# Input sums and part of the weight splits by accumulating transfers in a two-layer streaming encoder

## Chip, cores and metric

One core of one Trainium2 chip runs the whole program. The metric is the device time of one execution in microseconds (us); lower is better. Names of engines: PE is TensorE, DVE is VectorE, ACT is ScalarE, POOL is GpSimd, SP is SyncE (it issues the loads here).

## The reference, cut to what matters

Two token groups (512 prompt frames and 64 sample frames, 576 columns in all) go through two layers with shared weights, model width 1024, hidden width 2816. Every layer is a feed-forward block, a token mixer, and a second feed-forward block, each behind a norm whose shift, scale and gate come from a vector c per group:

```
mod = (silu(c) @ ada_w[l] + ada_b[l])          # shift, scale, gate for 3 sub-layers
hh  = rmsnorm(x) * (1 + scale) + shift
x   = x + 0.5 * gate * ((silu(hh @ w_gate) * (hh @ w_up)) @ w_out)     # feed-forward, twice in a layer
x   = x + gate * mixer(hh)      # layer 0: gated DeltaNet and short conv; layer 1: stick-breaking attention
```

So there are four feed-forward blocks; here they are called F0 (layer 0, first), F1 (layer 0, second), F2 (layer 1, first) and F3 (layer 1, second). Mixer 0 stands between F0 and F1, mixer 1 (the attention) between F2 and F3.

## The kernel before

**Precision by splitting.** Activations and weights are float32, each held as a high part rounded to the matrix unit's format and a low rest: XH, XL for a block's input (8 tiles of 128 rows, 576 columns), `wh`, `wl` for a weight tile. A product takes three matmuls, wh with XH, wh with XL, wl with XH, and runs over 288 columns (one half of the frames) at a time. `w_split` makes the pair: ACT copies the source into `wh`, and DVE subtracts, `wl = source - wh`.

**Pairs.** Weights come as 512 KB grains into three `stage` buffers, two grains to a pair. In a feed-forward block one pair is one gate tile and one up tile of 128 hidden units, over both halves of the frames. A plain pair (`dense`) takes 2 tiles x 8 row blocks x 2 halves x 3 = 96 matmuls.

**Seven-product pairs.** A pair can also be done by a fast 2x2 matrix scheme (`dense7`) with seven block products in place of eight: 7 x 4 x 3 = 84 matmuls, in the order P1, P2, P6, P5, P7, P3, P4. It needs sums of weight blocks (`w_sum`: four DVE operations into `ss`), four split weight tiles (`w_tile` 0 to 3; tile 0 serves P1 and P2, tile 1 P6 and P5, tile 2 P7 and P3, tile 3 P4) and four sums of input quarters, TH and TL, made once for each block by `t_task`. P6 adds into the PSUM bank in which P1 lay, so ACT's copy of P1 (`sg<-d`) has to be done before P6 starts. Tiles 0 to 2 of a pair are prepared during the products of the pair ahead, tile 3 after its own P1; the first seven-product pair behind a stretch of plain work prepares tiles 2 and 3 itself, after its P1.

`PLAIN = (22, 10, 10, 2)` says how many of a block's 22 pairs are plain, the first ones: F0 has no seven-product pair, F1 and F2 have 12 each, F3 has 20. A block's pairs go in chunks of 8, 8 and 6, and behind each chunk stands its part of the output product (source HH, HL). The first two pairs of a block run together in `start_sub`, and `t_task` is started behind them; it must be through (`S.finish(tt)`) before the first seven-product pair.

**Modulation.** `ada_task` computes `mod` on DVE: for each of the 144 tiles a 512 KB load `aw` and two fused multiply-and-sum operations (`jk<-aw,cb`), with `every` as the least distance between tiles. Layer 0's tiles but the first two groups are computed in F0, all 72 of layer 1 in F1 and F2.

**Order.** All engines run in program order. The order is made when the program is built: a table of engine clocks (`Model`) decides at each `S.tick()`, after every third matmul, which background task is stepped next.

Of the kernel before, what the change touches and what calls it, by code (L numbers as in the profile page):

```python
# [32 lines left out]
D = 1024  # L33
# [10 lines left out]
PK = ((1,5),(0,1))  # L44
LOLAG = 0
DSH = ((2, 4, 6), (1, 4, 6))
PLAIN = (22, 10, 10, 2)
EVEN_ODD = (0, 2, 4, 6, 1, 3, 5, 7)


# [241 lines left out]
def encoder_step(ctx: ExitStack, tc: tile.TileContext, a, o):  # L292
    nc = tc.nc
    M = Model()
# [43 lines left out]
    for n, sh in SMALL:  # L338
        k = 1
# [27 lines left out]
    def seven(i):  # L367

        return i < len(pairs) and pairs[i][0][0][2] == EVEN_ODD

    ss = {}
    spool = [None]
    HB = 4 * P

    def w_split(i, src, E=V):
        n = Model.size(src)
        h, l = wsp.tile([P, 1024], F32R, name="wh"), wsp.tile([P, 1024], F32R, name="wl")
        wt.setdefault(i, []).append((h, l))
        for c in range(0, n, HB):
            A.activation(h[:, c:c + HB], src[:, c:c + HB], AF.Copy)  # L380
        E.tensor_sub(l[:, :n], src, h[:, :n].bitcast(F32))

    def w_sum(i, n):

        g0, g1 = st[i, 0], st[i, 1]
        a11, a12, a21, a22 = g0[:, :HB], g0[:, HB:], g1[:, :HB], g1[:, HB:]
        if n in (1, 3):
            ss[i, n] = spool[0].tile([P, 1024], F32, name="ss", bufs=2)
        x1, x2 = ss[i, 1], ss.get((i, 3))
        if n == 1:  # L390
            V.tensor_add(x1[:, HB:], a21, a22)
        if n == 2:
            V.tensor_sub(x1[:, :HB], x1[:, HB:], a11)
        if n == 3:
            V.tensor_sub(x2[:, :HB], a11, a21)
        if n == 4:
            V.tensor_sub(x2[:, HB:], a12, x1[:, :HB])

    def w_tile(i, n):

        if n == 0:
            w_split(i, st[i, 0])
        if n == 1:
            w_split(i, ss[i, 1])
        if n == 2:
            w_split(i, ss.pop((i, 3)))
            ss.pop((i, 1))
            st.pop((i, 0))
            w_dma()
        if n == 3:  # L410
            w_split(i, st[i, 1][:, HB:])
            st.pop((i, 1))
            w_dma()

# [78 lines left out]
    def dense7(evac):  # L493
# [43 lines left out]
                evac(n, None)  # L537
        wt.pop(i)

    def t_task(pool):  # L540

        TH[0] = pool.tile([P, 4, 4, 288], F32R, name="TH")
        TL[0] = pool.tile([P, 4, 4, 288], F32R, name="TL")
        h0, h1 = slice(0, 288), slice(288, 576)
        Hf, Lf = XH.bitcast(F32), XL.bitcast(F32)

        def parts(n, k, t, E):
            A.activation(TH[0][:, n - 1, k], t, AF.Copy)
            E.tensor_sub(TL[0][:, n - 1, k], t, TH[0][:, n - 1, k].bitcast(F32))

        new = lambda: npool.tile([P, 288], F32, name="hf", bufs=5)
        for k in range(4):
            e, o = 2 * k, 2 * k + 1
            t1, b = new(), new()
# [3 lines left out]
            t2 = new()  # L558
            V.tensor_sub(t2, Hf[:, o, h1], t1)
            V.tensor_add(t2, t2, Lf[:, o, h1])  # L560
            yield S.clock + 300.0
            parts(2, k, t2, V)
            parts(1, k, t1, V)
            t3, d = new(), new()
            V.tensor_sub(t3, Hf[:, o, h1], Hf[:, e, h1])
            V.tensor_sub(d, Lf[:, o, h1], Lf[:, e, h1])
            V.tensor_sub(t2, Hf[:, o, h0], t2)
            V.tensor_add(t2, t2, Lf[:, o, h0])
            yield S.clock + 300.0
            V.tensor_add(t3, t3, d)  # L570
            parts(3, k, t3, V)
            parts(4, k, t2, V)
            yield S.clock + 300.0
# [168 lines left out]
    def ada_cond(pool):
        cb = pool.tile([P, 2, D], F32, name="cb")
        dma(cb, bass.AP(tensor=a["c"].tensor, offset=a["c"].offset, ap=[[0, P], [D, 2], [1, D]]))
        A.activation(cb, cb, AF.Silu)
        return cb
# [34 lines left out]
    def ffn(l, s, pool, task, out):  # L781
# [5 lines left out]
        def evac7(jj):  # L787
# [27 lines left out]
            def evac(step, ps):  # L815
                if step == "P1":
                    g[0] = copy("sg", ps, 3)
                n = {"P1": 0, "P2": 1, "P6": 2}.get(step, step)
                if step == "P6":
                    g[1] = copy("sg", ps, 3)  # L820
                if n in late:
                    late.pop(n)()
                if step == "P2":
                    V.tensor_add(g[0], g[0], ps)
                if step == "P5":
                    up[0] = copy("hm", ps, 2)
# [1007 lines left out]
```

## Time and profile before

| | |
|---|---|
| median of 3 runs | 2550.49 us (2549.56 to 2550.81) |
| the profiled execution | 2550.91 us, its span 2549.2 us |
| PE busy | 2384.6 us (94%), 18556 matmuls |
| DVE busy | 1791.0 us (70%) |
| ACT busy | 986.8 us (39%) |
| POOL busy | 353.6 us (14%) |
| DMA | 277.00 MB, mean 109 GB/s |

Matmuls overlap in the trace, so a busy PE says only that it had work; a stretch is judged by how many matmuls it holds. Stretches, in us from the span's start: F0 40 to 468, mixer 0 to 905, F1 to 1334, F2 to 1779, mixer 1 to 2120, F3 to the end.

### The profile page before, as it was taken

What the parts mean: (1) busy time and instruction counts of PE and PEld (TensorE: products, weight loads), DVE (VectorE), ACT (ScalarE), POOL (GpSimd) and SP (SyncE); (2) the same over time, 40 slices, a digit from 0 to 9 for tenths busy, and PEclk for the clock granted to TensorE, in tenths of its full rate; (3) what the DMA queues carried; (4) which work ended last, traced back from release to release, by engine and by line L of the source; (5) the groups of instructions that cost most, each with busy time, mean ns of one, the idle gap of its engine ahead of it and who ended that gap; (6) DMA issues with size and microseconds to landing.
All of it is one profiled execution on the core that took longest, in us unless ns stands there. A gap on an engine that the chain in (4) does not pass through costs nothing.

```text
span 2549.2 us, 46027 instructions
## 1 busy us (share of the span) xinstructions
PE 2384.6 (94%) x18556; PEld 2304.2 (90%) x18556; DVE 1791.0 (70%) x3528; ACT 986.8 (39%) x2015; POOL 353.6 (14%) x599
## 2 busy tenths in 40 slices
PE   6999999999998979989997998999999996999998
PEld 5999999988888969989896998999888886999998
DVE  7677776687775676687877658775656667748575
ACT  4322222543222432142443314344655544525352
POOL 4000000432222310000011000002333322000001
PEclk8999999998888989999998999999999998999999
DMA  6454443322122214344331443422222221223322
GB/s 236 158 173 160 173 158 131 120 77 55 32 65 90 102 67 157 116 141 141 133 123 67 149 149 116 130 77 92 88 72 84 66 83 34 91 83 93 98 82 81
DMA packets 95399, 277.00 MB, mean 109 GB/s; under 512 B 24738, under 2 KB 27042, under 8 KB 94804
## 3 DMA queue, kind: packets, MB, share of 16 engines
q1 hardware_dynamic: 95188, 274.07, 32.5%
q8 instruction: 146, 2.39, 0.4%
q14 instruction: 65, 0.53, 0.1%
HBM read 262.52 MB, written 11.51 MB: 107 GB/s over the span
## 4 chain that ended last, share of the span: by engine, by line
PE 70%; DVE 19%; ACT 5%; issue 3%; POOL 2%; DMA 1%; SPq 0%; DVEq 0%; ACTq 0%; POOLq 0%
PE d L191 61%; PE a L191 9%; DVE hf L191 3%; DVE wl L191 3%; DVE jk L191 2%; ACT wh L191 2%; DVE iz L191 1%; DVE ss L191 1%; DVE sg L191 1%; DVE cp L191 1%; ACT sg L191 1%; DVE TL L191 1%; DVE t2k L191 1%; DVE sy L191 1%; POOL sn L191 1%
## 5 line engine op out<-in xcount | busy, mean ns | idle before, releaser
L191 PE MATMUL d<-XH,wh 128*128 128x288 f32 x2832 | 869.8, 307 | 47.6 <-ACT sg L191 16.1
L191 PE MATMUL d<-XL,wh 128*128 128x288 f32 x2832 | 850.9, 300 | 16.1 <-POOL XL L191 9.5
L191 PE MATMUL d<-XH,wl 128*128 128x288 f32 x2832 | 847.7, 299 | 0.8 <-DVE wl L191 0.8
L191 PEld LDWEIGHTS d<-XH,wh 128*128 128x128 f32 x2832 | 544.6, 192 | 62.7 <-ACT sg L191 16.8
L191 PEld LDWEIGHTS d<-XL,wh 128*128 128x128 f32 x2832 | 545.3, 193 | 23.2 <-POOL XL L191 15.2
L191 PEld LDWEIGHTS d<-XH,wl 128*128 128x128 f32 x2832 | 544.3, 192 | 1.7 <-DVE wl L191 1.5
L191 DVE TENSOR_TENSOR wl<-stage,wh 128x1024 fp32r<-128x1024 f32 (+3 forms) x319 | 354.9, 1117 | 169.4 <-ACT wh L191 167.8
L191 ACT ACTIVATE wh<-stage 128x1024 fp32r<-128x1024 f32 (+3 forms) x389 | 334.6, 878 | 274.4 <-PE d L191 240.9
L191 PE MATMUL d<-HH,wh 128*128 128x288 f32 x1408 | 416.3, 296 | 0.0
L191 PE MATMUL d<-HL,wh 128*128 128x288 f32 x1408 | 416.0, 295 | 0.0
L191 PE MATMUL d<-HH,wl 128*128 128x288 f32 x1408 | 414.2, 294 | 0.3 <-DVE wl L191 0.3
L191 DVE SCALAR_TENSOR_TENSOR jk<-aw,cb 128x1024 bf16<-128x1024 f32 x272 | 339.2, 1247 | 4.8
L191 DVE SCALAR_TENSOR_TENSOR x<-d,mod,x 128x64 f32<-128x64 f32 (+2 forms) x384 | 146.7, 413 | 208.4 <-PE d L191 207.0
L191 POOL TENSOR_TENSOR acc<-acc,sq 128x288 f32<-128x288 f32 x72 | 58.4, 812 | 1653.3 <-ACT sq L191 1239.7
L191 PEld LDWEIGHTS d<-HH,wl 128*128 128x128 f32 x1408 | 264.5, 188 | 0.6 <-DVE wl L191 0.6
L191 PEld LDWEIGHTS d<-HL,wh 128*128 128x128 f32 x1408 | 264.2, 188 | 0.7 <-DVE HL L191 0.7
L191 PEld LDWEIGHTS d<-HH,wh 128*128 128x128 f32 x1408 | 264.1, 188 | 0.0
L191 PE MATMUL d<-TH,wh 128*128 128x288 f32 x704 | 214.2, 304 | 46.9 <-ACT sg L191 46.9
L191 PE MATMUL d<-TL,wh 128*128 128x288 f32 x704 | 212.4, 302 | 0.0
L191 PE MATMUL d<-TH,wl 128*128 128x288 f32 x704 | 212.1, 301 | 0.0
L191 ACT ACTIVATE HH<-hm 128x288 fp32r<-128x288 f32 x176 | 74.7, 445 | 295.1 <-DVE hm L191 295.1
L191 PEld LDWEIGHTS d<-TH,wh 128*128 128x128 f32 x704 | 136.9, 194 | 51.1 <-ACT sg L191 50.4
(319 smaller groups left out, 3181.6 us busy)
## 6 DMA issues: line engine op xcount, KB each, us to landing
stage<-in_w SPq DMA_DIRECT2D x301, 512.0 KB, 3.6
aw<-in_ada SPq DMA_DIRECT2D x136, 512.0 KB, 4.4
stage<-in_w SPq DMA_DIRECT2D x36, 384.0 KB, 3.1
stage<-in_w SPq DMA_DIRECT2D x8, 320.0 KB, 3.0
x<-in_x SPq DMA_DIRECT2D x4, 576.0 KB, 7.2
xd<-x SPq DMA_DIRECT2D x1, 2304.0 KB
x<-xd SPq DMA_DIRECT2D x1, 2304.0 KB
out_k<-kf SPq DMA_DIRECT2D x8, 288.0 KB, 4.4
```

Of the source, the lines that this page charges most:

```text
L191: r = real(*args, **kw)
```

## The change

- `t_task` no longer forms the four input sums on DVE (56 operations on 128x288). ACT copies four quarters of XH into TL, and ten accumulating transfers issued by POOL (`acc_dma`, a transfer that adds its source into its destination) add the other quarters to them. ACT then copies each sum to TH and DVE subtracts once for each quarter. The scheme's signs are turned so that only sums are needed; the weight sums change add for subtract. XH and XL are stored by quarters, so that a quarter is one run of 1152 elements in each partition.
- In F1 and F2 (`S2M`), the rests of weight tiles 2 and 3 are made by ACT and a transfer: ACT writes `wl = -source` rounded, and `acc_dma` adds the source.
- `PLAIN` becomes (22, 6, 6, 6): F1 and F2 get 16 seven-product pairs, F3 16.
- Modulation tiles: 48 in F0, 48 in F1 and F2 (as far as they reach), 24 in mixer 1, 8 in F3; `cb` (silu of c, broadcast) stays in place for the whole program, `aw` has fewer buffers. The output tile of the end shares its place with TH.
- The scratch of POOL's transfers grows from 512 to 2048 bytes.

```diff
-PLAIN = (22, 10, 10, 2)
+PLAIN = (22, 6, 6, 6)
...
-    XH = base.tile([P, 8, NT], F32R, name="XH")
-    XL = base.tile([P, 8, NT], F32R, name="XL")
+    XH = Quarters(base.tile([P, 2, 2, 4, 288], F32R, name="XH"))
+    XL = Quarters(base.tile([P, 2, 2, 4, 288], F32R, name="XL"))
+    cb = base.tile([P, 2, D], F32, name="cb")
...
-    def w_split(i, src, E=V):
+    def w_split(i, src, E=V, by_dma=False):
...
             A.activation(h[:, c:c + HB], src[:, c:c + HB], AF.Copy)
+        if by_dma:
+            A.activation(l[:, :n], src, AF.Copy, scale=-1.0)
+            acc_dma(l[:, :n].bitcast(F32), src)
+            return
         E.tensor_sub(l[:, :n], src, h[:, :n].bitcast(F32))
...
-            w_split(i, ss.pop((i, 3)))
+            w_split(i, ss.pop((i, 3)), by_dma=S2M[0])
...
-            w_split(i, st[i, 1][:, HB:])
+            w_split(i, st[i, 1][:, HB:], by_dma=S2M[0])
...
+    def acc_dma(out, in_):
+
+        nc.gpsimd.dma_start(out, in_, accum_op=OP.add)
+        M.issue("POOL", [out], [in_], 1000.0)
...
     def t_task(pool):
...
-            V.tensor_sub(t1, Hf[:, e, h1], Hf[:, e, h0])
-            V.tensor_sub(b, Lf[:, e, h1], Lf[:, e, h0])
-            V.tensor_add(t1, t1, b)
...
+        def parts(n):
+            A.activation(TH[0][:, n], Tf[n], AF.Copy)
+            V.tensor_sub(TL[0][:, n], Tf[n], TH[0][:, n].bitcast(F32))
+
+        for n, (par, half) in enumerate(((0, 0), (1, 1), (0, 1), (1, 0))):
+            A.activation(TL[0][:, n], H(par, half), AF.Copy)
+        yield S.clock
+        for x, y in ((L(0, 0), L(0, 1)), (H(0, 1), H(1, 1)), (L(0, 1), L(1, 1))):
+            acc_dma(Tf[0], x)
+            acc_dma(Tf[2], y)
+        acc_dma(Tf[1], L(1, 1))
+        acc_dma(Tf[3], L(1, 0))
+        acc_dma(Tf[1], Tf[0])
+        yield M.ready(Tf[2]) + 2000.0
+        parts(2)
+        yield M.ready(Tf[1]) + 1000.0
+        acc_dma(Tf[3], Tf[1])
+        yield S.clock + 2000.0
+        parts(0)
+        yield M.ready(Tf[3]) + 2000.0
+        parts(1)
+        yield S.clock + 2000.0
+        parts(3)
...
-        at = S.spawn(ada_task(ap, cb, [(0, j) for j in range(2, 9)], 5600.0))
+        at = S.spawn(ada_task(ap, [(0, j) for j in range(2, 8)], 6800.0, 3))
...
-        at = S.spawn(ada_task(ap, cb, [(1, j) for j in range(9)], 8500.0))
+        at = S.spawn(ada_task(ap, [(0, 8)] + [(1, j) for j in range(5)], 11000.0))
+        S2M[0] = True
...
+        at = S.spawn(ada_task(mp, [(1, j) for j in (5, 6, 7)], 12000.0, 1))
...
+        at = S.spawn(ada_task(fp, [(1, 8)], 8000.0))
```

The order in which the instructions now stand moves at three places. On DVE, behind the first plain pairs of F1, F2 and F3, the input sums stand in one row of operations (one of eight such pieces, before; `hf` is a scratch tile):

```order
L191 TENSOR_TENSOR hf<-XH 128x288
L191 TENSOR_TENSOR hf<-XL 128x288
L191 TENSOR_TENSOR hf<-hf 128x288
L191 TENSOR_TENSOR hf<-XH,hf 128x288
L191 TENSOR_TENSOR hf<-hf,XL 128x288
L191 TENSOR_TENSOR TL<-hf,TH 128x288 x2
```

In their place POOL's queue in F1 now holds the transfers that add, ten for TL and then two for each seven-product pair, where before it held nothing between the norm at the block's start and the one at its end:

```order
L560 DMA TL<-XL 128x1152 x2
L560 DMA TL<-XH 128x1152 x2
L560 DMA TL<-XL 128x1152 x4
L560 DMA TL<-TL 128x1152 x2
L560 DMA wl<-ss 128x1024
L560 DMA wl<-stage 128x512
```

So the sums have left DVE, and each waits in POOL's queue for the one it builds on. On ACT, one seven-product pair of F1 before, from the copy of P5's bank to the copy of the next P1's:

```order
L191 ACTIVATE hm<-d 128x288
L191 ACTIVATE sg<-sg 128x288
L191 ACTIVATE wh<-stage 128x512 x2
L191 ACTIVATE up<-d 128x288
L191 ACTIVATE wh<-ss 128x512 x2
L191 ACTIVATE sg<-sg 128x288
L191 ACTIVATE wh<-ss 128x512 x2
L191 ACTIVATE sg<-d 128x288
L191 ACTIVATE wh<-stage 128x512
```

and the same piece now:

```order
L191 ACTIVATE hm<-d 128x288
L191 ACTIVATE sg<-sg 128x288
L191 ACTIVATE wh<-stage 128x512 x2
L191 ACTIVATE up<-d 128x288
L191 ACTIVATE wh<-ss 128x512 x2
L191 ACTIVATE sg<-sg 128x288
L191 ACTIVATE wh<-ss 128x512 x2
L191 ACTIVATE wl<-ss 128x1024
L191 ACTIVATE sg<-d 128x288
L191 ACTIVATE wh<-stage 128x512
L191 ACTIVATE wl<-stage 128x512
```

Two copies `wl` came in, the long one ahead of the copy of P1. On DVE in the second chunk of F1, one pair now, from the product of the pair ahead to its weight tile 1:

```order
L191 TENSOR_TENSOR wl<-stage,wh 128x1024
L191 SCALAR_TENSOR_TENSOR jk,mod<-aw,cb 128x1024 x2
L191 TENSOR_TENSOR ss<-stage 128x512
L191 TENSOR_TENSOR ss<-stage,ss 128x512
L191 TENSOR_TENSOR up<-hm,up 128x288
L191 TENSOR_TENSOR sg<-d,sg 128x288
L191 TENSOR_TENSOR wl<-ss,wh 128x1024
L191 SCALAR_TENSOR_TENSOR jk,mod<-aw,cb 128x1024 x2
L191 TENSOR_TENSOR hm<-sg,up 128x288
```

Two modulation tiles stand in a pair there, one of them between weight tile 0 and the sums; before it was four tiles for three pairs.

## Rows read from the trace of the kernel before

**Rows 1.** Stretches of the trace: the bounds and length of each in us, then busy us of each engine with its count of instructions, the granted share of PE's clock, DMA's busy share and GB/s. In order: eight plain pairs (F0), the six seven-product pairs of F1's second chunk and of its third (the first with its P1 and P2 ahead of 1085), those of F2's second and third, and eight and six of F3.

```profile
199.10:301.00 101.90, 101.90 (x771) 101.90 (x770) 72.35 (x117) 27.52 (x46) 0.00 (x0) 1.00 0.47 161
1081.90:1163.20 81.30, 70.68 (x506) 68.72 (x505) 71.52 (x119) 38.64 (x86) 0.00 (x0) 0.98 0.40 136
1214.20:1293.50 79.30, 71.93 (x505) 70.20 (x505) 70.77 (x118) 37.94 (x86) 0.00 (x0) 0.96 0.39 133
1539.10:1620.70 81.60, 72.24 (x506) 70.29 (x506) 71.43 (x119) 38.86 (x86) 0.00 (x0) 0.96 0.41 135
1671.90:1738.50 66.60, 66.60 (x505) 66.60 (x504) 52.00 (x85) 38.35 (x86) 0.00 (x0) 1.00 0.31 96
2290.20:2379.00 88.80, 88.80 (x672) 88.80 (x671) 70.46 (x115) 51.97 (x115) 0.00 (x0) 1.00 0.33 101
```

**Rows 2.** PE's five long waits at the starts of F1, F2 and F3, from its timeline: start, length, what ran, and in brackets the idle time before it and what ended it.

```profile
930.77 0.61 PE L191 MATMUL d<-XH,wh 128*128 128x288 f32 x1 [7.69 <-ACT sg L191]
942.95 0.61 PE L191 MATMUL d<-XH,wh 128*128 128x288 f32 x1 [6.25 <-ACT wh L191]
1387.93 0.61 PE L191 MATMUL d<-XH,wh 128*128 128x288 f32 x1 [7.97 <-ACT sg L191]
1400.11 0.61 PE L191 MATMUL d<-XH,wh 128*128 128x288 f32 x1 [6.15 <-ACT wh L191]
2172.59 0.61 PE L191 MATMUL d<-TH,wh 128*128 128x288 f32 x1 [25.64 <-ACT sg L191]
```

**Rows 3.** Stretches around these waits, columns as in the first group.

```profile
923.00:960.00 37.00, 22.65 (x138) 21.98 (x138) 29.77 (x60) 11.62 (x25) 0.00 (x0) 0.77 0.23 75
1380.00:1417.00 37.00, 22.51 (x135) 21.92 (x136) 29.61 (x60) 11.78 (x25) 0.00 (x0) 0.77 0.22 74
2147.00:2181.00 34.00, 8.41 (x42) 8.41 (x43) 25.76 (x60) 10.77 (x27) 0.00 (x0) 0.60 0.10 31
```

**Rows 4.** Groups of DVE's instructions from 2143 to 2173 us, the start of F3's seven-product pairs: what, shapes and count, busy us and mean ns of one, idle us before them.

```profile
L191 DVE TENSOR_TENSOR TL<-hf,TH 128x288 fp32r<-128x288 f32 x16 | 6.6, 455 | 4.1 <-ACT TH L191 4.1
L191 DVE TENSOR_TENSOR hf<-hf,XL 128x288 f32<-128x288 f32 x8 | 3.7, 457 | 0.3
...
L191 DVE TENSOR_TENSOR hf<-XH 128x288 f32<-128x288 f32 x8 | 3.6, 452 | 0.0
```

**Rows 5.** ACT's timeline in one seven-product pair of F2's third chunk, in which no modulation tile runs; the first two rows are the copy of P5 and a silu, the last two the copy of the next pair's P1 and its tile 3.

```profile
1700.52 0.41 ACT L191 ACTIVATE hm<-d 128x288 f32<-128x288 f32 x1 [1.11 <-PE d L191]
1700.83 0.44 ACT L191 ACTIVATE sg<-sg 128x288 f32<-128x288 f32 x1
...
1705.54 0.45 ACT L191 ACTIVATE sg<-sg 128x288 f32<-128x288 f32 x1 [1.89 <-DVE sg L191]
1705.89 1.14 ACT L191 ACTIVATE wh<-ss 128x512 fp32r<-128x512 f32 x2
1706.93 0.39 ACT L191 ACTIVATE sg<-d 128x288 f32<-128x288 f32 x1
1707.22 0.62 ACT L191 ACTIVATE wh<-stage 128x512 fp32r<-128x512 f32 x1
```

**Rows 6.** DVE's timeline at that place, from weight tile 0 of the next pair to its tile 2.

```profile
1702.34 1.23 DVE L191 TENSOR_TENSOR wl<-stage,wh 128x1024 fp32r<-128x1024 f32 x1 [1.54 <-ACT wh L191]
1703.48 0.69 DVE L191 TENSOR_TENSOR ss<-stage 128x512 f32<-128x512 f32 x1
1704.08 0.68 DVE L191 TENSOR_TENSOR ss<-stage,ss 128x512 f32<-128x512 f32 x1
1704.69 0.45 DVE L191 TENSOR_TENSOR up<-up,hm 128x288 f32<-128x288 f32 x1
1705.06 0.45 DVE L191 TENSOR_TENSOR sg<-sg,d 128x288 f32<-128x288 f32 x1
1705.42 1.22 DVE L191 TENSOR_TENSOR wl<-ss,wh 128x1024 fp32r<-128x1024 f32 x1
1707.06 1.23 DVE L191 TENSOR_TENSOR wl<-ss,wh 128x1024 fp32r<-128x1024 f32 x1 [0.42 <-ACT wh L191]
```

**Rows 7.** PE's first matmul of P7 in that pair, from its timeline.

```profile
1700.32 0.29 PE L191 MATMUL d<-TH,wh 128*128 128x288 f32 x1
```

**Rows 8.** The same place in a pair of F1 in which a modulation tile runs: DVE's timeline.

```profile
1118.14 1.23 DVE L191 TENSOR_TENSOR wl<-stage,wh 128x1024 fp32r<-128x1024 f32 x1 [0.94 <-ACT wh L191]
1119.28 1.22 DVE L191 SCALAR_TENSOR_TENSOR jk<-aw,cb 128x1024 bf16<-128x1024 f32 x1
...
1121.69 0.69 DVE L191 TENSOR_TENSOR ss<-stage 128x512 f32<-128x512 f32 x1
```

**Rows 9.** What follows it: PE's first matmul of the next P6, from its timeline.

```profile
1125.58 0.40 PE L191 MATMUL d<-TH,wh 128*128 128x288 f32 x1 [2.08 <-ACT sg L191]
```

**Rows 10.** Groups of instructions over the whole span: ACT's copy of a whole weight tile, and POOL's sum of squares (what, shape and count, busy us and mean ns of one, idle before and what ended it).

```profile
L191 ACT ACTIVATE wh<-stage 128x1024 fp32r<-128x1024 f32 x213 | 221.6, 1050 | 236.6 <-PE d L191 203.1 <-issue 27.6 <-DMA stage<-in_w 3.6
...
L191 POOL TENSOR_TENSOR acc<-acc,sq 128x288 f32<-128x288 f32 x72 | 58.4, 812 | 1653.3 <-ACT sq L191 1239.7 <-PE d L191 399.6 <-issue 13.3
```

**Rows 11.** Transfers: the queue of SP's loads (packets, MB, share of 16 engines over the span), and the loads of 512 KB of weights (count, size, median us from issue to landing).

```profile
q1 hardware_dynamic: 95188, 274.07, 32.5%
...
stage<-in_w SPq DMA_DIRECT2D x301, 512.0 KB, 3.6
```

**Rows 12.** Mixer 1 as one stretch, columns as in the first group.

```profile
1779.00:2120.00 341.00, 321.22 (x2444) 293.21 (x2442) 216.58 (x466) 193.38 (x449) 125.17 (x283) 0.98 0.25 80
```

**Rows 13.** What PE waited for longest in that stretch: in total us, times, longest us.

```profile
PE a L191 <- DVE sg L191: 9.4, 24, 0.6
```

More of the change, by code (lines that the diff above doesn't have):

```diff
@@ L242, in free, with __init__, __getitem__ @@
         return self.m.free((id(self), name), bufs or self.bufs)
+class Quarters:
+    def __init__(self, t):
+        self.t = t
+    def __getitem__(self, at):
+        _, kt, r = at
+        half = r.start // 288
+        return self.t[:, half, kt % 2, kt // 2, r.start - 288 * half:r.stop - 288 * half]
 class Sched:
@@ L369, in seven @@
         return i < len(pairs) and pairs[i][0][0][2] == EVEN_ODD
+    S2M = [False]
     ss = {}
@@ L538, in dense7 @@
         wt.pop(i)
+    def acc_dma(out, in_):
+        nc.gpsimd.dma_start(out, in_, accum_op=OP.add)
+        M.issue("POOL", [out], [in_], 1000.0)
+        M.t["DMA"] = max(M.t["DMA"], M.t["POOL"] + 1300.0) + 4.0 * P * Model.size(out) / 150.0
+        M.mark([out], [in_], M.t["DMA"] + 700.0, "POOL")
     def t_task(pool):
@@ L543, in t_task @@
         TL[0] = pool.tile([P, 4, 4, 288], F32R, name="TL")
[L544 to L554, printed above, removed]
-            V.tensor_sub(t1, Hf[:, e, h1], Hf[:, e, h0])
-            V.tensor_sub(b, Lf[:, e, h1], Lf[:, e, h0])
-            V.tensor_add(t1, t1, b)
[L558 to L573, printed above, removed]
+        Tf = [TL[0][:, n].bitcast(F32) for n in range(4)]
+        H = lambda par, half: XH.t[:, half, par].bitcast(F32)
+        L = lambda par, half: XL.t[:, half, par].bitcast(F32)
+        def parts(n):
[20 more added lines that the diff above has]
+        parts(3)
     def dense_first(evacs, feed):
@@ L701, in encoder_step, with ada_dma @@
     aw = {}
-    def ada_dma(pool, todo):
+    def ada_dma(pool, todo, bufs):
         if todo:
             l, n = todo.pop(0)
-            aw[l, n] = pool.tile([P, D], F32, name="aw", bufs=3)
+            aw[l, n] = pool.tile([P, D], F32, name="aw", bufs=bufs)
             dma(aw[l, n], a["ada"][l, n])
@@ L727, in encoder_step, with ada_task @@
     hold = [False]
-    def ada_task(pool, cb, todo, every):
+    def ada_task(pool, todo, every, bufs=2):
         ahead = [(l, j * 8 + kt) for l, j in todo for kt in range(8)]
-        ada_dma(pool, ahead)
+        for _ in range(bufs - 1):
+            ada_dma(pool, ahead, bufs)
         yield S.clock + every
@@ L736, in ada_task @@
                     yield S.clock + 1000.0
-                ada_dma(pool, ahead)
+                ada_dma(pool, ahead, bufs)
+                if bufs == 1:
+                    yield S.clock + every - 3000.0
                 ada_tile(pool, cb, l, j, kt)
-                yield max(S.clock + every, M.t["DVE"] - 1000.0)
+                yield max(S.clock + (3000.0 if bufs == 1 else every), M.t["DVE"] - 1000.0)
             ada_end(l, j)
[L742 to L746, printed above, removed]
     def last_pairs(pool, l, s, ks, out):
@@ L830, in evac @@
                 if step == "P3":
-                    V.tensor_add(up[1], up[1], up[0])
-                    V.tensor_add(g[1], g[1], ps)
+                    V.tensor_sub(up[1], up[0], up[1])
+                    V.tensor_sub(g[1], ps, g[1])
                 if step == "P4":
@@ L1603, in final @@
         t0, t1 = HALF[half]
+        if not yo.get("y"):
+            yo["y"] = yo["pool"].tile([P, 4, 4, 288], F32, name="TH").rearrange("p a b c -> p (a b c)").rearrange(
+                "p (k t) -> p k t", t=NT)
         y = yo["y"]
@@ L1613, in encoder_step @@
         ap, fp = Ring(M, ap), Ring(M, fp)
-        first = fp.tile([P, 4, 4, 288], F32, name="TH").rearrange("p a b c -> p (a b c)")
-        crow = [first[0:1, g * D:(g + 1) * D] for g in range(2)]
+        crow = [ap.tile([P, D], F32, name="awp", bufs=3)[0:1] for _ in range(2)]
         for g in range(2):
@@ L1646, in encoder_step @@
         A.activation(cT, sm["cT"], AF.Silu)
-        cb = ap.tile([P, 2, D], F32, name="cb")
-        row = first[:, 2 * D:2 * D + P]
+        row = ap.tile([P, D], F32, name="awp", bufs=3)[:, :P]
         G.memset(row, 0.0)
```

15 lines of the change are left out of this document (8 added, 7 removed).

## The prediction

> **What bounds the kernel now.** I read the page's busy times first, then the stretches by matmul count, and then PE's waits in the feed-forward blocks. PE is the bound, and the question is where it isn't fed. Eight plain pairs of F0 take 101.9 us with no gap, 12.74 us for one, and 14 seven-product pairs of F2 and F3 take 66.6 and 88.8 us, 11.1 us for one [rows 1]. The same pairs beside modulation tiles take 81.3 and 79.3 us for six in F1, 81.6 in F2, 13.2 to 13.6 us each: slower than the plain pairs that they replace. DVE is then busy 71 of 80 us, against 52 of 66.6 without modulation. The reader is to see there that DVE sets those pairs, and not PE.
>
> The second place is the start of F1, F2 and F3. PE waits 7.69, 6.25, 7.97, 6.15 and 25.64 us for ACT [rows 2], and ACT stands behind DVE, which is making input sums: in 30 us at F3's start 40 operations of 0.45 us and 16 for the rests [rows 4]. PE's loss is more than the gaps, since its granted clock falls to 0.60 to 0.77 of full speed in these stretches, part of them at 1.2 of 2.4 GHz [rows 3]. With 0.132 us for a matmul (101.9 / 771 [rows 1]), the 138 matmuls of the first stretch are 18.2 us of work in 37, the 135 of the second 17.8 in 37, the 42 of the third 5.6 in 34 [rows 3]. Lost: 18.8 + 19.2 + 28.4 = 66.4 us.
>
> **The change, part by part.** The unknown is an accumulating transfer, of which the trace has none. I call D the time from the end of ACT's copy to the landing of 512 KB that PE can use. *Lower end:* a plain load of that size lands after 3.6 us [rows 11]. *Working value:* the load queue moved 274 MB in 32.5% of 2549 us, 331 GB/s when active, so 1.6 us of the 3.6 is data and 2.0 fixed. An add reads two operands for each one written, which I take as twice the data time, 3.2 us, so 5.2, and up to one short POOL operation of 0.81 us [rows 10] for preparing it: 5.2 to 6.0, I take 5.8. *Upper end:* with a load sharing the engines, another 1.6 us, and a second POOL operation, 8.
>
> *Input sums leave DVE.* Gain 66.4 us, if the new chain is ready in time. It has five adds one behind the other (three into the first quarter, then quarter one, then quarter three), 590 KB each, two of them often in flight together: 5 x 6.5 = 33 us at this D, with ACT's first copy, last copy and DVE's subtraction some 37. Its cover is four plain pairs, 51 us; in ACT's order the last copies stand in the fourth, about 3 x 12.74 + 3.2 = 41 us after the start. So it is hidden, just. What isn't hidden is ACT's four copies of 1152 columns in a row, 4 x 1.05 x 1152/1024 = 4.7 us [rows 10], ahead of the copies that free PE's banks; with four banks of 3.2 us most of it passes. I take 2 us for each block, **+6**; at D = 8 the chain is late by some 5 us in each, so up to +20, and at least 0.
>
> *F3's four pairs back to plain:* 4 x (12.74 - 11.1) = **+6.6**.
>
> *Rest of tile 2 by transfer.* In a clean pair the first matmul of P7 starts at 1700.32 [rows 7], DVE ends the sum for the gate at about 1705.45 [rows 6], ACT then does a silu and two copies, and starts the copy of the next P1 at 1706.93, 6.6 us after P7's start [rows 5]. The next P7 needs the rest after one pair and two matmuls, 11.1 + 0.3 = 11.4 us. Today DVE has it at 1708.29 [rows 6], 8.0 us, a slack of 3.4. Now ACT's negated copy follows at 6.6 and ends at 7.7, and the transfer has 3.7 us. At D = 5.8 it is 2.1 us late. A late P7 gives the time back to the next pair's chain, as this starts with P5's end and DVE reaches its wait for P3 1.2 us after P3's end, so the mean loss is (D - 3.7)/2 = 1.05 us. F2, 16 pairs with next to no modulation: 16 x 12.15 = 194.4, where before 81.6 + 66.6 + four plain pairs 51.0 = 199.2 [rows 1]: **-4.8**. At 3.6 it is 177.6 (-21.6); at 8, where the loss is D - 4.9, 227 (+28).
>
> *F1: modulation moves together.* The order now has two modulation tiles a pair in most of F1, and in about 11 of 16 pairs one stands between weight tile 0 and the sums. There it delays the copy of P1, and P6 waits for that copy: in the row of before, 2.41 us of modulation [rows 8] makes P6 wait 2.08 us [rows 9]. Now ACT's negated copy stands ahead of it too: 6.6 + 2.41 + 1.05 + 0.39 = 10.5 us after P7's start, and P6 and P5 take 3.2 more, 13.7 for the pair. DVE loses 1.8 us (1.23 for tile 2, half of it for tile 3) and gains 0.7 tiles, 1.7 us. So 11 x 13.7 + 5 x 12.15 = 211.5, before 81.3 + 79.3 + 51.0 = 211.6: **0**. Bounds: all pairs clean 177.6 (-34), all at 15 us 240 (+28).
>
> *First pairs.* The first of each chunk makes tile 2 behind its own P1: copy, two splits and the negation, 0.2 + 0.39 + 1.04 + 1.05 = 2.7 us, then D, while P7 needs it 5.0 us after P1's end (three products of 1.59 us and two matmuls). Late by D - 2.3 = 3.5 us, 2.4 more than the others, six times: **+14.4** (7.5 to 16).
>
> *Mixer 1* takes 24 tiles of 2.41 us, 58 us on a DVE that is busy 217 of 341 us; PE is 94% busy there [rows 12]. PE waits for DVE's product 9.4 us now [rows 13]; with DVE's idle share from 36% to 19% I double it: **+9** (0 to 24). The tiles left in F0, eight fewer, and those in F3's plain pairs stand beside plain pairs without a gap: 0 (F0's plain pairs in [rows 1] ran beside tiles at a closer spacing, 5600 against 8000 in the code, and lost nothing).
>
> Sum: -66.4 + 6 + 6.6 - 4.8 + 0 + 14.4 + 9 = -35. The profiled execution took 2550.9 us, its span 2549.2, the median of the runs 2550.5. 2550.9 - 35 = 2516, and I say 2517.
>
> **The rivals.** *The add is as quick as a load,* D = 3.6 to 4.5. For: landings of 3.6 us under traffic [rows 11]. Against: two operands. At 3.6: -66.4 + 1 + 6.6 - 21.6 - 5 + 7.5 + 9 = -69, 2482; at 4.5 about 2496. The Trainium skill (DMA: Bandwidth & Descriptors, "Anatomy of one DMA — SWDGE (gpsimd) path") fits a transfer issued by POOL with 2.0 us plus its bytes at 436 GB/s, an estimate of 3.2 us for 512 KB, by which the time would be about 2480; it speaks of copies, and no run here shows it.
>
> *The adds are slow and PE waits for the rests,* the other side. Place: P7 in the 32 pairs of F1 and F2. At D = 8: F2 +28, F1's pairs at 14.4 us +19, first pairs +15, chain +15, so -66.4 + 15 + 6.6 + 28 + 19 + 15 + 9 = +26, 2577. For: in F1 a pair now moves 1 MB of weights, up to 1 MB of modulation and 0.77 MB of adds, 3.2 + 3.2 + 4.7 = 11 us of transfer time at the rates above in a pair of 13.7, so they queue. Against: the loads of tile 3's buffer now start after its add has landed, out of the way. Between 5.8 and 8 the sum rises some 28 us for each us of D; it turns at D = 7.1.
>
> *The sums are not ready:* the ten adds and the loads beside them saturate the transfer engines (36 + 15 us of data in 51), ACT stands at the copy for TH some 10 us more, and the 66.4 us are half given back: 2550, no change.
>
> *POOL prepares its transfers late because DVE is in the way.* POOL and DVE would have to share a port, and each transfer would first wait for one of DVE's operations, up to 1.23 us [rows 6]. D would be 7.0 and the sum about -2: 2549, no change. POOL ran beside DVE in no seven-product pair so far (POOL 0.00 in [rows 1]), so no row speaks for or against it. The Trainium skill (SBUF — State Buffer, "SBUF: two separate sides", the "DVE blocks DMA" trap) states such a lock for DVE's two-port modes, which keep POOL from writing descriptors; the same page excepts operations on two tensors, and those are what DVE does here beside the transfers, so I give it little.
>
> **How the numbers follow.** Forecast, D from 4.5 to 6.7: 0.54. Quick adds: 0.16, all faster. Slow adds: 0.18. Sums late: 0.08. POOL held up: 0.04. A measurement of this kernel tells 0.2% (5 us) from no change. Faster: 0.54, 0.16, and 0.02 of the sums late: 0.72. Same: 0.03 of these and 0.03 of POOL: 0.06. Slower: 0.18, 0.03 and 0.01: 0.22. The range reaches from 2486 in the quick case to 2562 in the slow one; the likeliest's own is 2496 to 2541.
>
> **What would show it.** Right: no PE wait over 2 us at the starts of F1, F2, F3, and the granted clock near 1.0 there; F2's seven-product pairs at 11.5 to 12.5 us with PE waiting for wl landed by a transfer; F1's at 13 to 14 with waits for `sg`; first pairs of chunks 3 to 4 us longer. Wrong if the adds land outside 4.5 to 6.7 us, if ACT stands idle at the copies for TH, or if mixer 1 grows by more than 24 us.

## Time and profile after: the result

The changed kernel takes 2569.78 us (median of 8 runs, 2556.79 to 2574.89), the kernel before 2550.41 beside it: 1.007 of the time, interval 1.005 to 1.009. It is slower, by 19 us in the medians. The profiled execution took 2568.52 us, 17.6 more than that of the kernel before. From its page, the span, the busy times and the two queues of transfers (packets, MB, share of 16 engines):

```profile
span 2566.8 us, 46156 instructions
...
PE 2385.5 (93%) x18508; PEld 2301.0 (90%) x18508; DVE 1702.3 (66%) x3344; ACT 1050.9 (41%) x2090; POOL 453.7 (18%) x693
...
q1 hardware_dynamic: 95044, 273.02, 32.3%
q0 software_dynamic: 13536, 42.87, 9.1%
```

DVE has 89 us less to do, as was meant, and the span is longer. Where, the same four stretches show in both kernels: F1, F2 (each to the end of its last output product), mixer 1 and F3, a block counted from ACT's first copy of a full bank (bounds and length, busy us of PE, weight loads, DVE, ACT, POOL with counts, granted share of PE's clock, DMA share, GB/s). Before:

```profile
884.30:1334.50 450.20, 414.27 (x3005) 408.30 (x3004) 339.47 (x608) 156.41 (x315) 19.04 (x21) 0.97 0.37 126
1334.50:1778.80 444.30, 417.14 (x3062) 412.16 (x3061) 311.89 (x564) 163.69 (x327) 24.37 (x28) 0.97 0.34 112
1778.80:2122.40 343.60, 323.82 (x2463) 295.81 (x2463) 218.94 (x474) 195.06 (x451) 125.17 (x283) 0.99 0.25 79
2122.40:2549.00 426.60, 391.23 (x2925) 389.71 (x2923) 280.52 (x516) 179.38 (x382) 16.05 (x20) 0.96 0.26 81
```

After:

```profile
884.70:1340.40 455.70, 408.64 (x2956) 401.94 (x2955) 319.66 (x571) 195.48 (x374) 55.56 (x63) 0.97 0.60 168
1340.40:1768.50 428.10, 409.72 (x3015) 403.87 (x3014) 223.62 (x404) 201.80 (x387) 60.73 (x70) 0.99 0.49 126
1768.50:2146.90 378.40, 330.28 (x2464) 300.35 (x2463) 274.29 (x572) 194.44 (x451) 142.00 (x283) 0.94 0.32 107
2146.90:2566.00 419.10, 398.57 (x2973) 395.63 (x2971) 262.75 (x463) 168.96 (x338) 26.58 (x30) 0.98 0.36 106
```

F1 +5.5, F2 -16.2, mixer 1 +34.8, F3 -7.5; up to F1 the two agree within 0.4 us.

**The end of mixer 1.** The wait of [rows 13], for the product `sg` inside the attention, hardly grew: 11.4 us in all where it was 9.4. The one that grew is another, PE's wait for the residuals `x` that DVE adds in the last pairs (total us, times, longest us; before, then after):

```profile
PE d L191 <- DVE x L191: 2.6, 1, 2.6
...
PE d L191 <- DVE x L191: 22.3, 2, 19.7
```

Its long one is the third of these four gaps in PE's timeline (start, length, what ran, in brackets the idle time ahead and what ended it):

```profile
956.85 0.61 PE L191 MATMUL d<-XH,wh 128*128 128x288 f32 x1 [7.27 <-ACT wh L191]
...
982.20 0.61 PE L191 MATMUL d<-TH,wl 128*128 128x288 f32 x1 [6.82 <-DMA wl<-ss]
...
2117.31 0.58 PE L191 MATMUL d<-XH,wh 128*128 128x288 f32 x1 [19.73 <-DVE x L191]
...
2218.41 0.61 PE L191 MATMUL d<-XH,wh 128*128 128x288 f32 x1 [6.93 <-ACT wh L191]
```

What DVE does around that gap, from its timeline:

```profile
2094.39 1.22 DVE L191 SCALAR_TENSOR_TENSOR jk<-aw,cb 128x1024 bf16<-128x1024 f32 x1
...
2100.22 1.22 DVE L191 SCALAR_TENSOR_TENSOR jk<-aw,cb 128x1024 bf16<-128x1024 f32 x1 [3.34 <-DMA aw<-in_ada]
...
2105.98 1.22 DVE L191 SCALAR_TENSOR_TENSOR jk<-aw,cb 128x1024 bf16<-128x1024 f32 x1 [3.26 <-DMA aw<-in_ada]
...
2112.08 1.23 DVE L191 SCALAR_TENSOR_TENSOR jk<-aw,cb 128x1024 bf16<-128x1024 f32 x1 [3.60 <-DMA aw<-in_ada]
...
2116.66 1.78 DVE L191 SCALAR_TENSOR_TENSOR x<-d,mod,x 128x288 f32<-128x288 f32 x4
```

Four tiles stand in one row there, some 6 us each: 2.5 us of work and, for three of them, 3.3 to 3.6 of waiting, since with one buffer (`bufs` 1) a load starts only when the tile ahead has been used. The residuals `x<-d,mod,x`, which empty PE's banks, stand behind all four. Cut where the attention is through (2243 matmuls of the stage in both kernels, at 2089.0 before and at 2091.5 now), the 34.8 us are 12.8 beside the attention, which has 20 tiles, and 22.0 behind it, with these four. The clock that PE was granted is low around it, columns as above:

```profile
2073.00:2090.00 17.00, 13.16 (x50) 8.62 (x49) 12.19 (x24) 6.89 (x17) 5.35 (x15) 0.51 0.10 32
...
2100.00:2121.00 21.00, 3.69 (x15) 3.72 (x16) 11.70 (x21) 2.18 (x5) 2.40 (x3) 0.51 0.36 125
```

The second row lies in PE's wait; the first is the end of the attention, 50 matmuls in 17 us, where the kernel before gets through 140 at 1.00 (2070 to 2087). 0.51 is the lower of the clock's two levels or close to it, 1.2 of 2.4 GHz; in the 7 us before it fell, PE was busy for 4.83.

**The pairs.** The stretches that answer to [rows 1]: F1's second chunk (8 pairs) and third (6), F2's second and third:

```profile
1053.30:1166.80 113.50, 94.71 (x673) 92.37 (x673) 92.46 (x162) 64.26 (x131) 13.80 (x16) 0.97 0.74 196
1217.90:1300.10 82.20, 71.64 (x505) 69.89 (x505) 65.44 (x114) 46.86 (x98) 10.38 (x12) 0.96 0.75 198
1506.00:1603.00 97.00, 90.98 (x673) 89.26 (x672) 57.07 (x99) 63.58 (x131) 13.82 (x16) 1.00 0.64 153
1654.10:1728.20 74.10, 69.60 (x505) 68.41 (x505) 41.85 (x73) 47.08 (x98) 10.38 (x12) 0.98 0.61 149
```

14.2 and 13.7 us for a pair in F1, 12.1 and 12.35 in F2. PE's waits in the first of these stretches:

```profile
PE d L191 <- DMA wl<-ss: 17.1, 8, 3.6
PE d L191 <- ACT sg L191: 1.7, 2, 1.0
```

So a pair of F1 waits at P7 for the rest of tile 2 to land, and next to nothing at P6 for the copy of P1.

**The starts.** ACT's copies at the chain of adding transfers in F1, then in F3: the four into TL that begin it, and the first two to TH:

```profile
910.28 4.31 ACT L191 ACTIVATE TL<-XH 128x1152 fp32r<-128x1152 f32 x4
944.41 2.22 ACT L191 ACTIVATE TH<-TL 128x1152 fp32r<-128x1152 f32 x2 [7.07 <-DMA TL<-XL]
...
2172.18 4.32 ACT L191 ACTIVATE TL<-XH 128x1152 fp32r<-128x1152 f32 x4
2204.65 2.22 ACT L191 ACTIVATE TH<-TL 128x1152 fp32r<-128x1152 f32 x2 [5.40 <-DMA TL<-XL]
```

ACT stands idle for the chain, 7.07 us and 5.40, and 12 to 14 us later PE waits 7.27 and 6.93 us for ACT (the first and last of PE's gaps above). Between the two stands DVE: in F1 its second subtraction starts at 953.66, just as the ninth add lands (issued at 947.92, 5.7 us), which reads the quarter that the subtraction overwrites; the product `hm`, on which ACT's next copies wait, stands behind it.

### The profile page after: what moved, and what is told of

It is laid out like the page before. It is cut to its first block, busy times and chain, and to the rows that moved or that the text cites. A ratio compares the mean times of both kernels' runs of the same rounds, so it can differ in the third digit from the quotient of the medians.

```text
span 2566.8 us, 46156 instructions
## 1 busy us (share of the span) xinstructions
PE 2385.5 (93%) x18508; PEld 2301.0 (90%) x18508; DVE 1702.3 (66%) x3344; ACT 1050.9 (41%) x2090; POOL 453.7 (18%) x693
## 5 line engine op out<-in xcount | busy, mean ns | idle before, releaser
L191 PE MATMUL d<-XH,wh 128*128 128x288 f32 x2736 | 841.4, 308 | 52.5 <-DVE x L191 22.3
L191 PE MATMUL d<-XL,wh 128*128 128x288 f32 x2736 | 824.4, 301 | 11.4 <-POOL XL L191 9.9
L191 PE MATMUL d<-XH,wl 128*128 128x288 f32 x2736 | 822.6, 301 | 2.4 <-DVE wl L191 2.4
L191 PEld LDWEIGHTS d<-XH,wh 128*128 128x128 f32 x2736 | 528.2, 193 | 61.7 <-issue 26.2
L191 PEld LDWEIGHTS d<-XL,wh 128*128 128x128 f32 x2736 | 528.2, 193 | 23.4 <-POOL XL L191 16.3
L191 PEld LDWEIGHTS d<-XH,wl 128*128 128x128 f32 x2736 | 527.6, 193 | 3.8 <-DVE wl L191 3.5
L191 DVE TENSOR_TENSOR wl<-stage,wh 128x1024 fp32r<-128x1024 f32 (+3 forms) x287 | 331.1, 1159 | 193.4 <-ACT wh L191 191.7
L191 PE MATMUL d<-TH,wl 128*128 128x288 f32 x768 | 232.8, 303 | 44.0 <-DMA wl<-ss 44.0
L191 PE MATMUL d<-TL,wh 128*128 128x288 f32 x768 | 229.6, 299 | 0.0
L191 PEld LDWEIGHTS d<-TH,wl 128*128 128x128 f32 x768 | 147.5, 192 | 50.4 <-DMA wl<-ss 50.4
```

The lines of the kernel that those rows point to most:

```text
L191: r = real(*args, **kw)
```

## Experiments

All are judged by stages, since the whole scatters: what stands ahead of F1 took 870 to 891 us, and runs of the kernel before 2536 to 2560 beside these. In the profiled executions the difference lies in mixer 0, at PE's granted clock; the same 70 us in the kernel before and in the experiment `rests_dve` (the second gets through 60 matmuls more):

```profile
610.00:680.00 70.00, 67.20 (x712) 60.77 (x711) 54.31 (x152) 23.37 (x44) 13.92 (x33) 0.85 0.18 49
```

```profile
610.00:680.00 70.00, 66.84 (x772) 60.84 (x771) 61.81 (x172) 25.41 (x49) 18.77 (x37) 1.00 0.20 54
```

Stages of the profiled executions in us, cut as above (F3 start: to its first output product), and the time of all runs against the kernel before beside them, with its interval:

| | F1 | F2 | mixer 1 | F3 start | median | ratio |
|---|---|---|---|---|---|---|
| before | 450.2 | 444.3 | 343.6 | 116.6 | 2550.41 | |
| after | 455.7 | 428.1 | 378.4 | 109.3 | 2569.78 | 1.007 (1.005 to 1.009) |
| mix_two | 458.6 | 429.1 | 353.0 | 108.8 | 2547.93 | 0.9988 (0.997 to 1.0007) |
| mix_none | 458.6 | 431.2 | 342.4 | 108.6 | 2536.51 | 0.9923 (0.9892 to 0.9954) |
| mod_back | 456.4 | 444.7 | 343.9 | 99.5 | 2548.99 | 0.9983 (0.996 to 1.0007) |
| rests_dve | 435.2 | 419.1 | 379.6 | 109.8 | 2537.23 | 0.9944 (0.9928 to 0.996) |
| f12_sparse | 449.3 | 448.7 | 378.0 | 108.7 | 2583.76 | 1.0142 (1.0113 to 1.0171) |
| rests_dense | 461.4 | 405.1 | 380.3 | 108.2 | 2556.68 | 1.0025 (1.0003 to 1.0048) |
| sums_on_dve | 466.0 | 444.9 | 377.8 | 119.4 | 2596.07 | 1.0204 (1.0162 to 1.0245) |
| best | 436.8 | 422.4 | 343.5 | 97.2 | 2491.14 | 0.9782 (0.9749 to 0.9815) |
| best_hold | 429.4 | 430.0 | 342.1 | 98.8 | 2500.82 | 0.9791 (0.9771 to 0.9811) |
| best_hold_close | 437.0 | 420.4 | 343.3 | 99.5 | 2499.37 | 0.9777 (0.9745 to 0.9808) |

### Tiles in mixer 1: mix_two and mix_none

```diff
-at = S.spawn(ada_task(ap, [(0, j) for j in range(2, 8)], 6800.0, 3))
+at = S.spawn(ada_task(ap, [(0, j) for j in range(2, 8)] + [(1, 7)], 5600.0, 3))
...
-at = S.spawn(ada_task(mp, [(1, j) for j in (5, 6, 7)], 12000.0, 1))
+at = S.spawn(ada_task(mp, [(1, j) for j in (5, 6)], 12000.0, 1))
```

> Mixer 1 gets two of its three modulation groups, the third goes to F0. Theory A (mixer 1 loses in two places: some 22 us at its end, where five tiles are made one behind the other, each behind its own load, and some 20 us beside the attention): the end is freed, the attention keeps two thirds of its tiles. PE's wait of 19.7 us before the last pairs is gone, the attention's period goes from 36.7 us to about 36, mixer 1 is 25 to 30 us shorter, and the time is 2538 to 2548 us. F0 takes 8 tiles more at no cost. Theory B (mixer 1 loses by something else, the tiles are only where it shows): the wait moves to another product of DVE, the time stays at 2560 to 2570.

`mix_none` moves (1, 5) and (1, 6) to F0 as well (`every` 4300) and leaves out `S.finish(at)`.

> Mixer 1 has no modulation tile, all 24 go to F0. Theory A: the attention's period returns to the 33.9 us of the kernel before and the end is free: mixer 1 is some 45 us shorter, the time is 2520 to 2532 us, below that of the kernel before. If only the end counts, it stays with the kernel of two groups at 2540 to 2548. Theory B: 2555 or more, or F0 grows beyond 470 us from the span's start as DVE fills up there.

Mixer 1 with 16 tiles, and with none:

```profile
1776.00:2129.00 353.00, 39.92 (x64) 0.98 0.31 102
```

```profile
1776.00:2118.00 342.00, 320.38 (x2465) 292.10 (x2464) 218.13 (x468) 194.35 (x450) 126.05 (x283) 1.00 0.26 81
```

(The first row counts DVE's modulation alone.) Both places of theory A are there: 378.4 us, then 353.0, then 342.4. The second step is 16 tiles beside the attention, 10.6 us, 0.7 each. The first, 25.4, is the end and four tiles fewer beside the attention, which fits the 22 us above. Its sizes were off: the tiles cost 36 us in all, not 45, and without them the time is 2537, not 2520 to 2532. F0 took the 24 tiles at no cost that shows: it ends at 469.2, and at 468.0 to 469.3 in five executions with the changed kernel's tiles.

### Modulation as before: mod_back

The three calls of `ada_task` get the groups and spacings of the kernel before, and `aw` two buffers in F1 and F2.

> The modulation tiles lie as in the kernel before (72 in F1 and F2, none in mixer 1 and F3), the transfers stay. Mixer 1 is as short as without tiles (45 us less). F1 and F2 take 24 tiles more, 58 us of DVE, in pairs that wait for DVE and for the transfers in turn: if every tile in a seven-product pair delays the copy of P1 as in F1 now (13.7 to 14.2 us for a pair beside tiles, 12.1 without), F2's 16 pairs cost 25 to 30 us more and the time is 2545 to 2560. If the new pairs have room on DVE for a third tile, it is 2525 to 2535.

Mixer 1 is whole, and F2 takes 16.6 us more with 24 tiles more in both blocks: the dearer case, though less than the 25 to 30 that I gave it. What I had not asked for is in F3, whose eight tiles went too: its start is 99.5 us against 109.3. ACT's rows there:

```profile
2157.37 4.31 ACT L191 ACTIVATE TL<-XH 128x1152 fp32r<-128x1152 f32 x4
2186.18 2.22 ACT L191 ACTIVATE TH<-TL 128x1152 fp32r<-128x1152 f32 x2 [1.52 <-DMA TL<-XL]
```

From the first copy to the first TH 28.8 us without tiles, 32.5 with (2204.65 - 2172.18), and ACT's idle time falls from 5.40 to 1.52 us. The chain's six adds of XL land after 7.8 us there (median) and after 8.6 beside the tiles' loads, which share the transfer engines with them. Up to the first TH the chain is 3.7 of the 9.8 us; how the rest comes about isn't shown.

### Who makes the rests, and how many tiles stand beside: rests_dve, rests_dense, f12_sparse

`rests_dve` leaves out `S2M[0] = True`. `rests_dense` does too and spaces the tiles of F1 and F2 by 6500 for 11000; `f12_sparse` keeps the transfers and spaces by 17000. In `f12_sparse` F1's first residuals use a gate whose last modulation tiles come later.

> The rests of weight tiles 2 and 3 are made by DVE again in F1 and F2; all else as in the changed kernel. Theory C (the transfer's latency sets F2's pairs): F2's pairs go from 12.1 to 11.1 to 11.4 us (12 to 16 us less), the six first pairs lose 2.4 us less each (14 us less), F1's pairs, where DVE has 1.8 us more work beside two tiles, grow from 13.9 to 14.2 to 14.8 us (5 to 15 us more): 2550 to 2560 us. Rival: DVE was full in F1 and the transfers are what lets 16 pairs run there: F1's pairs at 15.5 us or more, the time 2570 to 2590.

> All rests by DVE, and the tiles of F1 and F2 closer (6500 for 11000 in the code): two tiles in a seven-product pair of F1, as in the changed kernel with transfers. Theory A (crowded tiles): DVE has 11.8 us of work in a pair and the tiles stand ahead of what PE waits for, so F1's pairs take 13.5 to 14.5 us where they took 12.3 to 12.5 with one tile, F1 is 15 to 25 us longer than there, F2 2 to 6 us shorter (no tiles left), the time 2543 to 2558 us. Theory B (the transfers): the pairs stay near 12.5, the time near 2535.

> The changed kernel with the modulation tiles of F1 and F2 further apart (17000 for 11000 in the code, in the planner's own time): a seven-product pair of F1 then holds 1.1 tiles, not 1.9; eleven or so tiles more go to F2. Rests still by transfer. Theory A (the crowded tiles are what a pair of F1 pays for, the transfer costs 1 us a pair as in F2): F1's pairs take 12.4 to 13.0 us where they took 14.2 and 13.7, F1 is 14 to 22 us shorter, F2 some 5 to 10 us longer, the time 2552 to 2563 us. Theory B (the transfers are what a pair of F1 pays for, as they queue behind loads): F1's pairs stay at 13.5 to 14.2, the time at 2566 to 2574.

One chunk of eight pairs: with DVE and 8.5 tiles (`rests_dve`, F1), with DVE and 15.5 (`rests_dense`, F1), by transfer and 8 tiles (`f12_sparse`, F2):

```profile
1032.80:1131.20 98.40, 91.27 (x673) 89.36 (x673) 89.19 (x147) 51.04 (x115) 0.00 (x0) 1.00 0.42 133
```

```profile
1062.10:1180.70 118.60, 97.94 (x673) 94.18 (x672) 106.78 (x178) 51.47 (x115) 0.00 (x0) 0.96 0.43 141
```

```profile
1506.80:1616.40 109.60, 94.84 (x673) 92.40 (x673) 76.33 (x133) 63.43 (x131) 13.83 (x16) 0.97 0.66 168
```

With the rows of the section on the result, and 88.8 us for DVE without tiles [rows 1], eight pairs take

| rests | no tile | 8 to 8.5 tiles | 15 to 15.5 tiles |
|---|---|---|---|
| by DVE | 88.8 | 98.4 | 118.6 |
| by transfer | 97.0 | 109.6 | 113.5 |

The cells stand in different blocks, and by transfer they scatter: 96.7 to 101.1 without tiles (F2 of `mix_two`, `mix_none` and `sums_on_dve`), 108.8 to 116.0 with 15 (F1 of `mod_back`, `mix_two` and `mix_none`). Both theories hold a part. Tiles cost 1.1 to 1.9 us each on either side. The transfer costs 8 to 12 us for eight pairs as long as DVE has room, and gains 3 to 10 only where two tiles stand in each pair. None of the three did what I wrote in full. `rests_dve` is faster than both of its cases: its pairs in F1 take 12.3 us, not 14.2 to 14.8, and it gained 29.5 us in F1 and F2. The reason is in the builder: its table of clocks prices a rest by transfer dearly (`acc_dma`'s last two lines) and gives a pair of F1 some 24 us, with DVE 12.7; so the same `every` puts 15 tiles into a chunk where it puts 8.5 with DVE. `rests_dense` has theory A's time, but its pairs at 14.8 us and F1 at 26.2 longer lie above its bounds, and F2 is 14.0 shorter where 2 to 6 was written. `f12_sparse` is slower than both of its cases, and its pairs of F1, at 13.4, are nearer to theory B. The crowding of F1 came with `S2M`, not with 11000. `f12_sparse` shows that spacing alone doesn't help: what F1 gains (6.4 us), F2 loses (20.6), and the pairs of F2, clean before, pay for its tiles and the transfer at once.

### The input sums by themselves: sums_on_dve

```diff
-        for x, y in ((L(0, 0), L(0, 1)), (H(0, 1), H(1, 1)), (L(0, 1), L(1, 1))):
-            acc_dma(Tf[0], x)
...
+            V.tensor_add(t1, Hf[:, e, h1], Hf[:, e, h0])
+            V.tensor_add(b, Lf[:, e, h1], Lf[:, e, h0])
+            V.tensor_add(t1, t1, b)
```

> The changed kernel with the input sums on DVE again, in the new signs: 48 additions of 128x288, then copies and subtractions in 16 pieces each, no adding transfer at the blocks' starts. Theory A (the sums were a loss of 66 us in the three starts and the chain of transfers gives back about two thirds of it): each start is 10 to 20 us longer than in the changed kernel, the time 2600 to 2620 us. Theory B (the chain of ten transfers costs PE as much as DVE's sums did): the starts stay within 5 us, the time within 2562 to 2580.

F1, F2 and F3's start are longer by 10.3, 16.8 and 10.1 us, 37 in all, the medians by 26: theory A, with 2596 us just short of its 2600 (the profiled executions differ by 21.5 only, as what stands ahead of F1 was 15 us shorter in this one). The chain is worth having, at somewhat over half of what I had taken it for.

### The parts that pay together: best, best_hold, best_hold_close

```diff
+at = S.spawn(ada_task(ap, [(0, j) for j in range(2, 8)] + [(1, j) for j in (5, 6, 7)], 4300.0, 3))
...
+at = S.spawn(ada_task(ap, [(0, 8)] + [(1, j) for j in (0, 1, 2, 3, 4, 8)], 10000.0))
-        S2M[0] = True
...
-                S.finish(at)
```

> Input sums by transfer as in the changed kernel; all rests by DVE; 72 tiles in F0, 56 in F1 and F2 at 10000 in the code, none in mixer 1 and none in F3. If the parts add up: F1 437 us from its first copy to its end, F2 420 to 428, mixer 1 343, F3's start 99 to 101 (its eight tiles cost it 9 us), which beside the kernel before's 450, 444, 344 and 117 is some 50 to 55 us less: 2495 to 2503 us. If the tiles in F1 and F2 cost the starts of these blocks more, 2505 to 2520.

2491 us, 0.978 of the kernel before (0.9749 to 0.9815): the stages came out within 3 us of what was written, and the median lies 4 below it (the profiled execution, with the stages above, took 2500.82). The two that follow stop the tiles while a chain is under way (`ada_task` waits on a flag that `t_task` holds); F1's gate is used there, too, before its last tiles are made.

> As the kernel named best, but no modulation tile is made while a block's input sums are under way (from the first adding transfer to the last subtraction), so that four plain pairs of F1 and of F2 stand without tiles; the tiles go to the pairs and the output products behind. Theory A (a tile beside the plain pairs of a start is not free: it stands ahead of DVE's work for the sums, and PE then waits for ACT): the starts of F1 and F2, 112.7 and 119.7 us in best, come to 100 to 107 each, PE's wait for wh there falls from 7.3 and 6.3 us to under 3, F2's second chunk gets 8 tiles and takes 5 to 8 us more, the time is 2470 to 2482 us. Theory B (the chain of transfers alone sets the starts): they change by less than 4 us, the time is 2488 to 2500.

> The same with the tiles closer, 8500 for 10000 in the code: one in every pair of F1, fewer left for F2. A pair with one tile and rests by DVE takes 12.3 to 12.6 us against 11.1 without, wherever it stands, so moving four tiles from F2 to F1 changes the time by less than 4 us either way from the kernel with 10000; if F1's output products pay for the tiles too, it is 4 to 8 us slower.

Between the theories: up to their first output product F1 and F2 take 106.6 and 115.4 us, not 112.7 and 119.7, ACT's idle time at the first TH of F1 falls from 7.29 to 2.33 us and PE's wait from 7.3 to 4.3. So the tiles, with their loads, make some 5 us of the chain, and the rest is its own. F1's start still has 4.3 us where F3's, without tiles, has 1.5 in `best`: the second subtraction stands 38.7 us behind the first add there, and 36.1 in F3. The first two adds already land later in F1, 7.8 and 8.9 us against 6.1 and 6.7; why is left open. But the tiles pay elsewhere: F2's second chunk goes from 93.5 to 103.6. No gain in the time. Closer tiles move 8 to 10 us from F2 to F1, and the time stays, as expected.

## Why the prediction was wrong, point by point

**Mixer 1, "+9 (0 to 24)", is the step that failed:** +34.8, beyond its own bound. I sized it by doubling PE's wait for DVE in [rows 13], a wait inside the attention, as if all 24 tiles were spread beside it. There 20 of them cost 12.8 us, near what I said but not by that wait, which went from 9.4 to 11.4. The other 22 us came from where the stage ends, which I had not priced at all: by the builder's clocks the tiles come 12 to 14 us apart, four were left at the end, and `S.finish(at)` put them in one row ahead of the residuals, with a single buffer. Both stand in the diff, and the row of tiles stands in DVE's new order; I read the order in F1 and not there.

**F3's tiles, "0":** 9.8 us (`mod_back`). I called them free because F0's are [rows 1]. But F0's plain pairs have no chain of adds beside them. F3's start was forecast at -19.8 (-28.4 + 2 + 6.6) and gave -7.3.

**What the chain leaves, "2 us for each block":** the first wait is 7.27 us in F1 and 1.4 in F2. In F1 the chain's first adds took 34.1 us to the first TH (944.41 - 910.28); I had 37 for the whole chain, and 2.2 us of copies and two more transfers were still to come. I took 6.5 us for an add. Landings, F1 first, then F2 (count, size, median us from issue to landing):

```profile
aw<-in_ada SPq DMA_DIRECT2D x46, 512.0 KB, 4.8
wl<-ss POOLq DMA_DIRECT2D x16, 512.0 KB, 5.6
...
TL<-XL POOLq DMA_DIRECT2D x6, 576.0 KB, 10.7
...
TL<-TL POOLq DMA_DIRECT2D x2, 576.0 KB, 5.6
```

```profile
wl<-ss POOLq DMA_DIRECT2D x16, 512.0 KB, 4.6
...
TL<-XL POOLq DMA_DIRECT2D x6, 576.0 KB, 7.0
```

With no other add in flight an add takes 5.6 us, less than I took; with several in flight, beside loads, 7 to 10.7. And the subtraction that holds DVE until the ninth add has landed was in no sum of mine. The rival "the sums are not ready" named this wait, with 8 in 100. It was part of the truth beside the larger miss in mixer 1.

**D, 5.8 us:** right for the rests. ACT's copy in F1 ends at 1070.38, POOL starts 0.36 us later, and the landing takes 4.6 (F2) to 5.6 us (F1) from there, 5.0 to 6.0 in all:

```profile
1069.34 1.04 ACT L191 ACTIVATE wl<-ss 128x1024 fp32r<-128x1024 f32 x1
```

```profile
1070.74 0.86 POOL L560 DMA_DIRECT2D wl<-ss  x1 [11.15 <-ACT wl L191]
```

So neither the quick nor the slow adds came, and POOL wasn't held up behind DVE, which was busy 92.46 of 113.5 us around it. (In F1's second chunk alone the median landing is 6.0 us; the slowest is F1's first rest, 8.4.) The Trainium skill's fit (DMA: Bandwidth & Descriptors, "Anatomy of one DMA — SWDGE (gpsimd) path") gives an estimate of 3.2 us for the size; it is a fit for copies, and this trace has 4.6 for an add.

**F2, -14.8:** right, -16.2, and in its parts: -13.8 up to its first output product, where -14.8 was forecast, and -2.3 for 0 in the two later chunks. Its pairs at 12.15 took 12.1 and 12.35, with the first pairs among them. But the comparison that I didn't make says more: without the transfers, as without tiles, these pairs are at 11.1 (`rests_dve`: 88.9 us for eight). In F2 the rests by transfer are a loss of 1.0 us a pair, by my own sum.

**F1's pairs, "0":** 14.2 and 13.7 against 13.7 in 11 and 12.15 in 5. The size is near by luck, since the wait is another. I had P6 waiting for the copy of P1; that is 1.7 us in eight pairs, and the landing of tile 2's rest, at P7, is 17.1. In one of these pairs ACT's silu waits 2.74 us for DVE's product, the negated copy ends at 1085.35, POOL starts the transfer at 1085.71, and PE goes on at 1091.8, 6.1 us later. So the delay on DVE and the transfer stand in one chain, where I had priced them apart.

**First pairs, "3.5 us late":** PE waits 2.3 to 2.8 us for the rest in five of the six, and 6.82 in F1's first.

The misses in us: mixer 1 +25.8, F3's start +12.5, F1 +15.1 (-9.6 forecast, +5.5 measured; 9.0 of it up to its first output product, 5.1 in the two later chunks), F2 -1.4: 52, and 2516 + 52 is 2568, the profiled time. All three signs of being wrong showed: the chain's adds outside 4.5 to 6.7 us, ACT idle at the copies for TH, and mixer 1 up by more than 24.

## What to carry to other kernels

Work that has room on an engine's busy share still has a price by place. The same tile cost nothing that shows beside F0's plain pairs, 0.6 to 0.7 us beside the attention, 1.2 in the start of F3, 1.1 to 1.9 in a seven-product pair, and 5.5 in the row at the end of mixer 1, where it waited for its own load. When background work is moved, look in the new order at the place where it must be finished, and count what is left there and its buffers. And price each of two bundled edits against the best neighbour, not against the kernel before: here the input sums by transfer were worth 37 us, and mixer 1, F3's tiles and the rests by transfer took more than that.

## What I had not expected of the hardware

An adding transfer of 576 KB within the chip's own memory lands after 5.6 us with no other add in flight, and after 10.7 us (median) with others and loads beside it. And the clock that PE is granted in mixer 0 differs between executions of kernels whose instructions there are the same (0.85 and 1.00 in the same 70 us): mixer 0 took 416.2 us in the first and 402.2 in the second. What decides it no run here shows.
